# All large tiles 48 bytes past the weights modulo 256

## The chip, the cores and the metric

The kernel runs on one core of one Trainium2 chip. The metric is the device time of one execution in microseconds; three runs of the kernel before gave 1348.78 (median), 1347.21 and 1349.9 us. The runs themselves thus lie within 0.2% of each other.

## What is computed

One inference step of a streaming encoder layer for 256 prompt tokens and 32 sample tokens, which the kernel keeps side by side as 288 columns. The reference, cut to the parts that set the work:

```python
h = rmsnorm(x, norm_in)
(a_q, a_k, a_v, i_q, i_k, i_w, a_z, b_z, b_xbc, b_dt, m_q, m_z, gates) = split_cols(h @ w_in)
...
ya = dsa_attention(...) * jax.nn.silu(a_z)
yb, conv_state, h_last = mamba_branch(b_z, b_xbc, b_dt, ...)
ym = mem_attend(m_q, mem_k, mem_v) * jax.nn.silu(m_z)
g_a, g_b, g_m = jnp.split(jax.nn.sigmoid(gates), N_BRANCH, axis=-1)
merged = g_a * (ya @ w_pa) + g_b * (yb @ w_pb) + g_m * (ym @ w_pm)
return x + merged @ w_o, (k_new, v_new, i_k, conv_state, h_last)
```

Before it, 256 memory tokens are normalised and multiplied by `w_mem_kv`. Everything is float32. All weights together are some 207 MB (395 loads of 512 KB), each read once.

## The kernel before

**Products of three terms.** Each float32 operand of a large product is split into a high part, rounded to the matmul's input format (`F32R`), and a low part, the rest. A product is then high by high, low by high and high by low, accumulated in PSUM: three matmuls for each 128x128 block of weights. The weights are the stationary operand, the 288 token columns the moving one.

**Strips.** `strip` makes 128 output channels. Its weights come in halves of 8 blocks (512 KB): SyncE loads them into `wr` (line 217), ScalarE rounds them into `wh` (line 231), VectorE writes the rest into `wl` (line 232), with three buffers of each (`wpool`). `convert` issues these for the next half while TensorE works on the present one. The 24 matmuls of a half stand in this order: for the rows 0, 2, 4, 6, 1, 3, 5, 7 of the moving tile first `wh` by the high row and `wh` by the low row, then, with the rows in the opposite order, `wl` by the high row. A weight load precedes each matmul, so while a matmul streams its moving row, the weights of the next one are loaded.

**Which tiles are high and low rows.** `xh` and `xl` hold the normed input for `w_in`; slots E and F hold the gated outputs of the memory branch and of attention (`ym`, `ya`), A and B that of the Mamba branch (`yb`), `xh` and `mgl` (in the place of `xl`) the merged result for `w_o`. In the stage of the memory tokens, B and C hold the memory rows (256 columns); there `mv_block` has the memory as the stationary operand and 512 columns of weights as the moving one.

**Side work.** Attention, the scan and the norms are generators that run a step after each half; their matmuls write the PSUM tiles `sd`, those of the strips `ps`. All matmuls are issued by `mm` (line 78).

**Addresses.** A row of a moving tile is 1152 bytes long, four and a half times 256; the two halves of a weights tile (even and odd blocks) lie 2176 bytes apart, eight and a half times 256, and a block is 512 bytes. A row and the weights of the same parity thus have the same distance modulo 256 throughout a tile. `slot` shifts a tile by SHIFT bytes behind its start in the pool. Where the tiles start, modulo 256, as the built programs place them (per partition):

| tile | before | after |
|---|---|---|
| `wh`, `wl` (start of the first block) | 224 | 80 |
| high rows: `xh`, A, E | 128 | 128 |
| low rows: `xl`/`mgl`, B, F | 160 | 128 |
| memory rows in B and C | 160 | 16 |
| high rows minus weights | 160 | 48 |
| low rows minus weights | 192 | 48 |
| memory rows minus weights | 192 | 192 |

Of the kernel before, what the change touches and what calls it, by code (L numbers as in the profile page):

```python
# [7 lines left out]
F32 = mybir.dt.float32  # L8
F32R = mybir.dt.float32r
# [4 lines left out]
P = 128  # L14
# [19 lines left out]
def step_kernel(ctx, tc, ins, outs):  # L34
# [4 lines left out]
    const = ctx.enter_context(tc.tile_pool(name="const", bufs=1))  # L39
    wpool = ctx.enter_context(tc.tile_pool(name="wpool", bufs=3))  # L40
# [20 lines left out]
    def st(n=8):  # L61
        return stp.tile([P, n], F32, tag="st", name="st")

    SHIFT = {"A": 160, "B": 32, "E": 224, "F": 32}

    def slot(tag, shape, dt=F32):

        o = SHIFT.get(tag, 0) // 4
        n = {"E": 2304, "F": 2304, "G": 2304, "H": 2304}.get(tag, 4608)
        t = big.tile([P, n + o], dt, tag=tag, name=tag)  # L70
        m = 1
        for d in shape[1:]:
            m *= d
        t = t[:, o:o + m]
        return t if len(shape) == 2 else t.rearrange("p (a b) -> p a b", a=shape[1])
# [4 lines left out]

    N = Names()
    N.memraw = slot("A", [P, 16, 256])
    N.memh = slot("B", [P, 16, 256], F32R)
    N.meml = slot("C", [P, 16, 256], F32R)
    N.x = slot("D", [P, 16, T])
    def high():
        return const.tile([P, 4616], F32R, name="xh", tag="xh")[:, 0:4608].rearrange("p (k t) -> p k t", k=16)

    xh = high()
    xl = const.tile([P, 16, T], F32R, name="xl", tag="xl")  # L90
    X = (xh, xl)
# [2 lines left out]
    g_mem = const.tile([P, 16], F32, name="g_mem")  # L94
    S.dma_start(g_mem, ins["cols"][:, 0:16])
    nc.sync.dma_start(N.memraw[:, 0:1], ins["memT"][:, 0:1])
    cols = const.tile([P, 288], F32, name="cols")
    g_in, g_ssm, g_fin, d_col = (cols[:, 16 * i:16 * i + 16] for i in range(1, 5))
    cw = cols[:, 80:176].rearrange("p (c i) -> p c i", c=24)
    cbias = cols[:, 176:200]  # L100
# [103 lines left out]
    def convert():  # L204
        i = state["c"]
        if i >= len(jobs):
            return
        state["c"] += 1
        ap, shape, go = jobs[i]
        if ap is None:  # L210
            if shape == "now":
                go()
            else:
                conv.append((None, None, go))
            return convert()
        raw = wpool.tile(shape, F32, tag="wr", name="wr")
        nc.sync.dma_start(raw, ap)
        wh = wpool.tile([P, 1088], F32R, tag="wh", name="wh")
        wl = wpool.tile([P, 1088], F32R, tag="wl", name="wl")
        if shape == [P, 8, P]:  # L220


            wh, wl = (bass.AP(tensor=w.tensor, offset=w.offset, ap=[w.ap[0], [544, 2], [P, 4], [1, P]])
                      for w in (wh, wl))
            raw = raw.rearrange("p (k e) c -> p e k c", e=2)
        elif len(shape) == 3:
            wh, wl = (w[:, 0:shape[1] * shape[2]].rearrange("p (a b) -> p a b", b=shape[2]) for w in (wh, wl))
        else:
            wh, wl = (w[:, 0:shape[1] * shape[2] * shape[3]].rearrange("p (a b c) -> p a b c", a=shape[1], b=shape[2])
                      for w in (wh, wl))  # L230
        S.activation(wh, raw, AF.Copy)  # L231
        V.tensor_tensor(wl, raw, wh.bitcast(F32), OP.subtract)  # L232
        conv.append((wh, wl, go))
# [56 lines left out]
    def run():  # L290
        while conv:
            wh, wl, go = conv.pop(0)
            if wh is None:
                go()
                continue
            convert()
            go(wh, wl)
            step()
# [114 lines left out]

    mem_split(0, 1)
    convert()
    mem_load(1, 1)
    mem_split(1, 1)
    convert()
    mem_load(2, 2)
    mem_split(2, 2)  # L420
# [694 lines left out]
    def begin_pb():  # L1115
        N.mg = (high(),
                const.tile([P, 16, T], F32R, name="mgl", tag="xl"))
# [149 lines left out]
```

## Time and profile before

| | |
|---|---|
| median of three runs | 1348.78 us |
| the profiled execution | 1347.85 us, its span 1346.1 us |
| TensorE matmul busy | 1328.0 us, 99% of the span |
| TensorE weight loads busy | 1296.4 us, 96% |
| VectorE, ScalarE, GpSimd busy | 57%, 46%, 16% |
| granted TensorE clock | 0.997 of full on the mean |
| HBM traffic | 171 GB/s over the span |

[...]

### The profile page before, as it was taken

The page shows a single profiled execution, that of the slowest core. Times are in us where ns is not written, and L with a number is a line of the kernel's source. Part 1 is how long each engine was busy: PE and PEld are TensorE (multiplying, and loading weights), DVE is VectorE, ACT ScalarE, POOL GpSimd, SP SyncE. Part 2 cuts the span into 40 slices and gives each one's busy share as a digit, 9 for nine tenths or more (in the row PEclk, how much of TensorE's full clock was granted, in tenths as well). Part 3 has the DMA queues.
Part 4 walks back from the last instruction along what each step waited for, and adds up shares of the span by engine and source line. Part 5 has one row for each costly group of instructions (what it writes and reads, how often), then busy time and mean ns, then how long its engine had stood idle before and what let it go on. Part 6 is the DMA issues. An engine that isn't in the chain of part 4 may idle for free.

```text
span 1346.1 us, 24533 instructions
## 1 busy us (share of the span) xinstructions
PE 1328.0 (99%) x10102; PEld 1296.4 (96%) x10102; DVE 763.2 (57%) x1175; ACT 624.3 (46%) x871; POOL 209.0 (16%) x291
## 2 busy tenths in 40 slices
PE   9999999999999999999999999999999999999996
PEld 9889999899999999999999999999999999999995
DVE  6874434584577767646566546763344444555444
ACT  6654443444555544735435346664333434334331
POOL 0001000000012212122231234510012000000552
PEclk9999999999999999999999999999999999999998
DMA  8767343344444444655546444444446544445442
GB/s 296 259 210 259 131 141 126 130 157 171 158 142 145 154 157 165 227 168 175 186 141 193 167 163 166 160 169 172 162 169 233 172 167 172 167 164 173 169 162 100
DMA packets 64815, 232.05 MB, mean 172 GB/s; under 512 B 7552, under 2 KB 8224, under 8 KB 63424
## 3 DMA queue, kind: packets, MB, share of 16 engines
q1 hardware_dynamic: 60800, 212.25, 45.7%
q0 software_dynamic: 3328, 16.91, 3.7%
q8 instruction: 79, 1.29, 0.4%
q10 hardware_dynamic: 576, 1.34, 0.3%
q14 instruction: 32, 0.26, 0.1%
HBM read 223.06 MB, written 7.33 MB: 171 GB/s over the span
## 4 chain that ended last, share of the span: by engine, by line
PE 93%; DVE 2%; DMA 2%; issue 1%; ACT 1%; DVEq 0%; SPq 0%; ACTq 0%
PE ps L78 85%; PE sd L78 7%; DMA wr<-in_w_mk 2%; DVE wl L232 1%; ACT wh L231 1%; PE sd L932 0%; DVE A L1161 0%; DVE ev L385 0%; PE sd L798 0%; PE sd L506 0%; PE sd L916 0%; ACT t L661 0%; DVE E L346 0%; DVE t L610 0%; DVE xl L141 0%
## 5 line engine op out<-in xcount | busy, mean ns | idle before, releaser
L232 DVE TENSOR_TENSOR wl<-wr,wh 128x1024 fp32r<-128x1024 f32 (+1 forms) x395 | 487.3, 1235 | 539.9 <-ACT wh L231 530.3
L231 ACT ACTIVATE wh<-wr 128x1024 fp32r<-128x1024 f32 (+1 forms) x395 | 416.2, 1056 | 598.3 <-PE ps L78 467.1
L78 PE MATMUL ps<-xh,wh 128*128 128x288 f32 x2384 | 644.4, 298 | 0.0
L78 PE MATMUL ps<-xl,wh 128*128 128x288 f32 x2128 | 567.0, 293 | 0.2 <-DVE xl L141 0.2
L78 PEld LDWEIGHTS ps<-xh,wh 128*128 128x128 f32 x2384 | 448.7, 188 | 7.5 <-issue 5.5
L78 PEld LDWEIGHTS ps<-xl,wh 128*128 128x128 f32 x2128 | 401.4, 189 | 1.7 <-issue 0.7
L78 PE MATMUL ps<-xh,wl 128*128 128x288 f32 x2384 | 361.0, 293 | 0.0
L78 PEld LDWEIGHTS ps<-xh,wl 128*128 128x128 f32 x2384 | 327.8, 188 | 0.0
L78 PE MATMUL ps<-B,wh 128*128 128x288 f32 (+1 forms) x320 | 77.0, 291 | 0.0
L78 PE MATMUL ps<-E,wh 128*128 128x288 f32 x256 | 69.2, 298 | 0.0
L78 PE MATMUL ps<-A,wh 128*128 128x288 f32 x256 | 68.3, 294 | 0.0
L78 PE MATMUL ps<-mgl,wh 128*128 128x288 f32 x256 | 68.2, 293 | 0.0
L78 PE MATMUL ps<-F,wh 128*128 128x288 f32 x256 | 68.2, 293 | 0.0
L861 POOL COPY cso<-t 128x3 f32<-128x3 f32 x24 | 23.1, 961 | 237.8 <-ACT t L859 237.8
L78 PEld LDWEIGHTS ps<-B,wh 128*128 128x128 f32 x320 | 56.3, 189 | 0.0
L78 PEld LDWEIGHTS ps<-E,wh 128*128 128x128 f32 x256 | 48.2, 188 | 1.1 <-issue 0.8
L78 PEld LDWEIGHTS ps<-F,wh 128*128 128x128 f32 x256 | 48.3, 189 | 0.2 <-issue 0.2
L78 PEld LDWEIGHTS ps<-mgl,wh 128*128 128x128 f32 x256 | 48.3, 189 | 0.0
L78 PEld LDWEIGHTS ps<-A,wh 128*128 128x128 f32 x256 | 48.2, 188 | 0.0
L78 PE MATMUL ps<-E,wl 128*128 128x288 f32 x256 | 38.7, 293 | 0.0
L78 PE MATMUL ps<-A,wl 128*128 128x288 f32 x256 | 38.7, 293 | 0.0
L78 PEld LDWEIGHTS ps<-E,wl 128*128 128x128 f32 x256 | 35.2, 188 | 0.0
(302 smaller groups left out, 1149.1 us busy)
## 6 DMA issues: line engine op xcount, KB each, us to landing
wr<-in_w_in SPq DMA_DIRECT2D x266, 512.0 KB, 3.3
wr<-in_w_pb SPq DMA_DIRECT2D x32, 512.0 KB, 3.3
wr<-in_w_o SPq DMA_DIRECT2D x32, 512.0 KB, 3.2
wr<-in_w_mv SPq DMA_DIRECT2D x16, 512.0 KB, 4.3
wr<-in_w_pm SPq DMA_DIRECT2D x16, 512.0 KB, 3.2
wr<-in_w_pa SPq DMA_DIRECT2D x16, 512.0 KB, 3.2
wr<-in_w_mk SPq DMA_DIRECT2D x15, 512.0 KB, 5.1
B<-scr POOLq DMA_DIRECT2D x4, 1152.0 KB, 9.6
```

What stands on the lines that cost most here:

```text
L78: PE.matmul(out, lhsT, rhs, start=start, stop=stop)
L231: S.activation(wh, raw, AF.Copy)
L232: V.tensor_tensor(wl, raw, wh.bitcast(F32), OP.subtract)
L861: G.tensor_copy(cso[:, c, 0:3], u[:, 256:259])
```

## The change

The weights tiles are read and written from their fifth element on (16 bytes in), the pads of the slots go except one of 64 bytes before A, that of `xh` goes, and `cols` grows by 128 bytes, all of which moves what is allocated behind them. The memory rows in B and C are taken from the slots' 37th element on. No instruction is added, removed or moved on any engine; only addresses differ.

```diff
-    SHIFT = {"A": 160, "B": 32, "E": 224, "F": 32}
+    SHIFT = {"A": 64}
...
-    N.memh = slot("B", [P, 16, 256], F32R)
-    N.meml = slot("C", [P, 16, 256], F32R)
+
+    N.memh, N.meml = (slot(t, [P, 4608], F32R)[:, 36:4132].rearrange("p (k t) -> p k t", k=16) for t in "BC")
...
-        return const.tile([P, 4616], F32R, name="xh", tag="xh")[:, 0:4608].rearrange("p (k t) -> p k t", k=16)
+        return const.tile([P, 4608], F32R, name="xh", tag="xh")[:, 0:4608].rearrange("p (k t) -> p k t", k=16)
...
-    cols = const.tile([P, 288], F32, name="cols")
+    cols = const.tile([P, 320], F32, name="cols")
...
-        wh = wpool.tile([P, 1088], F32R, tag="wh", name="wh")
-        wl = wpool.tile([P, 1088], F32R, tag="wl", name="wl")
+        wh = wpool.tile([P, 1088], F32R, tag="wh", name="wh")[:, 4:1060]
+        wl = wpool.tile([P, 1088], F32R, tag="wl", name="wl")[:, 4:1060]
```

## Rows read from the trace of the kernel before

**Rows 1.** The page: engine, busy us, share, instructions; then the granted clock.
```profile
PE 1328.0 (99%) x10102; PEld 1296.4 (96%) x10102; DVE 763.2 (57%) x1175; ACT 624.3 (46%) x871; POOL 209.0 (16%) x291
...
PEclk9999999999999999999999999999999999999998
```

**Rows 2.** The chain that ended last: shares by line, then its pieces (start, us).
```profile
PE ps L78 85%; PE sd L78 7%; DMA wr<-in_w_mk 2%; DVE wl L232 1%; ACT wh L231 1%; PE sd L932 0%; DVE A L1161 0%; DVE ev L385 0%; PE sd L798 0%; PE sd L506 0%; PE sd L916 0%; ACT t L661 0%; DVE E L346 0%; DVE t L610 0%; DVE xl L141 0%
...
279.38 69.23 PE ps L78 x528
...
884.97 446.88 PE ps L78 x3408
```

**Rows 3.** The page's costliest groups: matmuls of 288 columns, with their counts.
```profile
L78 PE MATMUL ps<-xh,wh 128*128 128x288 f32 x2384 | 644.4, 298 | 0.0
L78 PE MATMUL ps<-xl,wh 128*128 128x288 f32 x2128 | 567.0, 293 | 0.2 <-DVE xl L141 0.2
...
L78 PE MATMUL ps<-xh,wl 128*128 128x288 f32 x2384 | 361.0, 293 | 0.0
...
L78 PE MATMUL ps<-E,wh 128*128 128x288 f32 x256 | 69.2, 298 | 0.0
```

**Rows 4.** Groups by form in 885 to 1331 us: busy us, mean ns.
```profile
L78 PE MATMUL ps<-xh,wh 128*128 128x288 f32 x752 | 200.8, 295 | 0.0
L78 PE MATMUL ps<-xl,wh 128*128 128x288 f32 x496 | 132.1, 293 | 0.0
L78 PE MATMUL ps<-xh,wl 128*128 128x288 f32 x747 | 113.1, 293 | 0.0
L78 PE MATMUL ps<-B,wh 128*128 128x288 f32 x256 | 68.2, 293 | 0.0
```

**Rows 5.** Single low-row matmuls: groups by form at 563.76, 564.46, 564.72, 565.64 us.
```profile
L78 PE MATMUL ps<-xl,wh 128*128 128x288 f32 x1 | 0.3, 298 | 0.0
...
L78 PE MATMUL ps<-xl,wh 128*128 128x288 f32 x1 | 0.3, 290 | 0.0
...
L78 PE MATMUL ps<-xl,wh 128*128 128x288 f32 x1 | 0.3, 294 | 0.0
...
L78 PE MATMUL ps<-xl,wh 128*128 128x288 f32 x1 | 0.3, 291 | 0.0
```

**Rows 6.** The same at 1008.53 and 1008.79 us, then at 1326.34 and 1326.60 us.
```profile
L78 PE MATMUL ps<-F,wh 128*128 128x288 f32 x1 | 0.3, 290 | 0.0
...
L78 PE MATMUL ps<-F,wh 128*128 128x288 f32 x1 | 0.3, 293 | 0.0
...
L78 PE MATMUL ps<-mgl,wh 128*128 128x288 f32 x1 | 0.3, 290 | 0.0
...
L78 PE MATMUL ps<-mgl,wh 128*128 128x288 f32 x1 | 0.3, 293 | 0.0
```

**Rows 7.** Two consecutive `wl` matmuls each, at 566.03 and 566.16 us.
```profile
L78 PE MATMUL ps<-xh,wl 128*128 128x288 f32 x2 | 0.4, 294 | 0.0
...
L78 PE MATMUL ps<-xh,wl 128*128 128x288 f32 x2 | 0.4, 293 | 0.0
```

**Rows 8.** Groups by form at 30 to 39.5 us, 42 to 52 us, 60 to 95 us.
```profile
L78 PE MATMUL ps<-B,wh 128*128 128x256 f32 x26 | 3.6, 276 | 0.0
...
L78 PE MATMUL ps<-B,wh 128*128 128x256 f32 x27 | 3.8, 281 | 0.0
...
L78 PE MATMUL ps<-wh,B 128*128 128x512 f32 x24 | 9.4, 392 | 0.0
L78 PE MATMUL ps<-wl,B 128*128 128x512 f32 x26 | 7.1, 391 | 0.0
```

**Rows 9.** Groups of VectorE, then ScalarE, at 900 to 1300 us, and a DMA issue.
```profile
L232 DVE TENSOR_TENSOR wl<-wr,wh 128x1024 fp32r<-128x1024 f32 x127 | 155.6, 1225 | 210.9 <-ACT wh L231 206.2 <-ACT D L1111 2.3 <-ACT H L1093 2.3
...
L231 ACT ACTIVATE wh<-wr 128x1024 fp32r<-128x1024 f32 x128 | 135.4, 1058 | 212.1 <-PE ps L78 180.6 <-issue 27.3 <-DMA wr<-in_w_in 4.0
...
wr<-in_w_in SPq DMA_DIRECT2D x266, 512.0 KB, 3.3
```

**Rows 10.** SyncE's DMA queue: what it waited for (us in total, times, longest).
```profile
SPq L217 <- DVE wl L232: 973.8, 340, 6.4
```

## The prediction

> **What bounds the kernel.** [...] Next the chain that ended last: 85% of it is one line, the strips' matmuls into `ps`, and hardly a wait for another engine stands in it [rows 2]. So what a strip matmul costs is what the kernel costs, and the question is what sets that cost. The length of a record does not tell it, since records overlap; the pieces of the chain do. One holds 3408 matmuls in 446.88 us, another 528 in 69.23 us: 131.1 ns from start to start in both [rows 2]. [...] In the first of these stretches the records are 293 to 295 ns long on the mean [rows 4]; a record is thus its interval plus 162.5 ns, and I turn the lengths of single records into intervals with that.
>
> Nothing else is near the bound. A half strip (24 matmuls) takes 24 x 131.1 = 3147 ns. For it ScalarE needs 1058 ns and VectorE 1225 ns [rows 9], and both wait for TensorE; SyncE's loads wait for the buffers to come free, 340 times [rows 10], not for data: a load lands 3.3 us after its issue [rows 9], with three buffers to hide it. Even intervals of 127 ns, 3048 ns a half, leave these covers in place.
>
> **The change part by part.** No instruction is added, removed or moved, so no queue, no wait and no buffer changes. Three things move: the distance of moving rows to weights, the start of `wh` and `wl` for the engines that write them, and the start of most small tiles.
>
> The small tiles (`t2`, `ev`, the attention and scan tiles) and the DMA targets shift by multiples of 16 bytes. I cost that at nothing. What hides it is TensorE's lead: VectorE is busy 57% and ScalarE 46% [rows 1]. If their work on a half rose by a fifth, some 0.46 us, 2.28 would become 2.74 us, still below 3.05 us. The side matmuls are 7% of the chain [rows 2]; they keep their mutual distances for the greater part, and I leave them.
>
> The distance is the change. The matmuls of 288 columns number 8688: 2384, 2128 and 2384 in the three big groups and seven groups of 256 (one of the seven stands in [rows 3]). While one streams its row, the next one's weights are loaded, so the distance that can matter is the row streaming now minus the weights loading now. In a half of 24 it is, before, 160 for the high rows and 192 for the low ones, with two exceptions where the order passes between even and odd rows: the low row 6 meets weights of the other parity and stands at 64, and in the `wl` part one high row stands at 32. After the change 22 of the 24 stand at 48, the two exceptions at 176. So 8688 x 22/24 = 7964 intervals change their distance to 48, and 724 move to a place between the two that they know, which I cost at nothing.
>
> No row has 48. All distances of the large tiles before are multiples of 32, and 48 is an odd multiple of 16. The nearest on either side are just the two exceptions. At 64 the record is 290 ns [rows 5, 6] (the second row of the one, the first and third of the other), which is an interval of 127.5 ns; it is so in each of the three tile pairs, while the next low row, two starts later, has 293 or 294, 130.5 to 131.5 ns. At 32 there are only means of two, since `wl` records of one group overlap: 294 with the record before it and 293 with the one behind [rows 7], which makes some 131 ns; I take 130.5 for it, since the pair's other half stands at 160 and high. Between 127.5 and 130.5 I take the middle, 129.0, because 48 is as far from the one as from the other. **The sum:** (131.1 - 129.0) x 7964 = 16.7 us less. The end at 64's value is 3.6 x 7964 = 28.7 us less, the end at 32's value 0.6 x 7964 = 4.8 us less. Against the profiled execution, 1347.85 us (its span is 1346.1; the rest lies around it and stays), that is 1331.1, with 1319.2 and 1343.1 as ends. The median of the runs is 0.9 us above the profiled one, so the forecast is **1332 us**, in its own case 1314 to 1344.
>
> [...]
>
> **The rivals.** *The distance is not what sets the interval.* The low rows at one and the same distance, 192, show 298, 294 and 291 ns [rows 5], so place in the sequence counts as much as distance; and in the memory stage, at 192 throughout and with the same code, the record goes from 276 to 281 ns after a short pause at 40 us and stays there [rows 8]. [...] That speaks for a rhythm between loads and streams into which the engine falls whatever the addresses. The time would be 1348 us, within 0.2% (the measure of what can be told from no change here). [...] *The change does not do what it says* is no case apart: the built addresses do stand at 48.
>
> [...]
>
> **How the numbers follow.** Faster by way of a shorter interval: 0.50, since the two nearest distances in the same sequence both lie at or below the mean. The same: 0.22, for the rhythm that ignores the addresses. Slower: 0.28, for the only steady run at a near distance, which has the largest excess of all. Likeliest is the first, 1332 us. The range runs from 1314 to 1366: it leaves out some 0.03 below and the upper half or a little more of the slower case, 0.16. Faster by over 0.2% (below 1346.1) 0.50, within 0.2% 0.22, slower 0.28.
>
> **What would show it.** In the profile after, the chain's long piece of 3408 matmuls should last 3408 x 129.2 = 440 us in place of 446.88, and the records of all 288-column groups should be some 291 ns; low row 6 should lose its short record. [...] VectorE's and ScalarE's lengths for `wl` and `wh` should stay at 1225 and 1058 ns; if they moved much, the start at 80 would count for itself. In the memory stage nothing should change, its distance being the same; if the records of 276 ns there become 281 or the reverse, the rhythm is set by something other than the distance. The prediction is wrong if the records of the `wl` part, where all have one distance before and after, do not move with those of the `wh` part.

## The result, and the profile after

The changed kernel takes 1360.3 us (median of four runs, 1359.98 to 1361.2) where the kernel before takes 1348.0 (1347.11 to 1349.9): a ratio of 1.0084, interval 1.0072 to 1.0096. It is 12 us slower; the forecast was some 16 us faster. The range, 1314 to 1366 us, does hold the time, but on the side of the rival that I gave 0.28.

The page of the profiled execution after: its span, engines (busy us, share, instructions), granted clock, and the groups that answer to [rows 1, 3] (busy us, mean ns of one record, idle before).

```profile
span 1358.3 us, 24529 instructions
...
PE 1338.0 (99%) x10102; PEld 1306.7 (96%) x10102; DVE 763.0 (56%) x1175; ACT 625.7 (46%) x871; POOL 209.1 (15%) x291
...
PEclk9999999999999999999999999999999999999998
...
L78 PE MATMUL ps<-xh,wh 128*128 128x288 f32 x2384 | 648.9, 298 | 0.0
L78 PE MATMUL ps<-xl,wh 128*128 128x288 f32 x2128 | 571.8, 295 | 0.2 <-DVE xl L141 0.2
...
L78 PE MATMUL ps<-xh,wl 128*128 128x288 f32 x2384 | 365.0, 295 | 0.0
```

TensorE is busy 10.0 us longer with the same 10102 matmuls, and the span is 12.2 us longer. The granted clock has not moved: it is 0.997 of full on the mean in both. VectorE and ScalarE are busy as long as before, to within 1.4 us, and their groups at 900 to 1300 us, answering to [rows 9], have the lengths of before to the nanosecond:

```profile
L232 DVE TENSOR_TENSOR wl<-wr,wh 128x1024 fp32r<-128x1024 f32 x127 | 155.6, 1225 | 211.2 <-ACT wh L231 211.1
...
L231 ACT ACTIVATE wh<-wr 128x1024 fp32r<-128x1024 f32 x127 | 134.4, 1058 | 208.5 <-PE ps L78 174.7 <-issue 28.3 <-DMA wr<-in_w_in 5.2
```

So no engine got more work, and the time is in the matmuls themselves. The pieces of the chain that ended last show how much each takes (start us, us, what).

```profile
280.92 69.96 PE ps L78 x528
...
892.42 451.58 PE ps L78 x3408
```

Before, the long piece took 446.88 us [rows 2]; now 451.58. That is 132.5 ns from start to start in place of 131.1, and the piece of 528 says the same (69.96/528 = 132.5). The difference, (451.58 - 446.88)/3408 x 8688 = 12.0 us, is nearly the whole loss. Two smaller differences beside it almost cancel: TensorE idles some 2.1 us longer in the first 60 us (the span grew by 12.2 us, its busy time by 10.0), and the matmuls of the memory stage and of the side work take 1.7 us less, by their starts in the two traces. That idle time lies between 2.1 and 4.3 us in the nine traces of whole kernels, of fast and slow layouts alike; why it varies was not tested.

The groups by form at 892 to 1332 us, answering to [rows 4], then two low rows, answering to the second and third of [rows 5] (565.60 and 565.87 us).

```profile
L78 PE MATMUL ps<-xh,wh 128*128 128x288 f32 x725 | 194.9, 295 | 0.0
L78 PE MATMUL ps<-xl,wh 128*128 128x288 f32 x496 | 133.2, 295 | 0.0
L78 PE MATMUL ps<-xh,wl 128*128 128x288 f32 x720 | 110.2, 295 | 0.0
L78 PE MATMUL ps<-B,wh 128*128 128x288 f32 x256 | 68.8, 295 | 0.0
...
L78 PE MATMUL ps<-xl,wh 128*128 128x288 f32 x1 | 0.3, 294 | 0.0
...
L78 PE MATMUL ps<-xl,wh 128*128 128x288 f32 x1 | 0.3, 298 | 0.0
```

The records of the low rows (`wh` part) and those of the `wl` part have both grown by 2 ns; those of the high rows in the `wh` part have stayed at 295. Low row 6 has lost its short record (290 before, 294 now). So the addresses do act. But the stage of the memory tokens has changed too, where weights and rows kept their distance of 192 (groups by form at 30 to 39.5, 42 to 52 and 60 to 95 us):

```profile
L78 PE MATMUL ps<-B,wl 128*128 128x256 f32 x27 | 3.7, 275 | 0.0
...
L78 PE MATMUL ps<-B,wh 128*128 128x256 f32 x32 | 4.4, 279 | 0.0
L78 PE MATMUL ps<-C,wh 128*128 128x256 f32 x31 | 4.2, 275 | 0.0
L78 PE MATMUL ps<-B,wl 128*128 128x256 f32 x24 | 3.2, 275 | 0.0
...
L78 PE MATMUL ps<-wh,B 128*128 128x512 f32 x25 | 9.7, 388 | 0.0
L78 PE MATMUL ps<-wl,B 128*128 128x512 f32 x28 | 7.5, 388 | 0.0
```

After the short pause only five records are still some 281 ns (with a first one of 363 they raise the mean of one group to 279); the others are 275 or 276. Those of 512 columns have fallen from 391 or 392 to 388 ns [rows 8]. That was the sign, named ahead, that something other than the distance sets the interval. The experiments ask what.

### The profile page after: what moved, and what is told of

It is laid out like the page before. It is cut to its first block, busy times and chain, and to the rows that moved or that the text cites. A ratio compares the mean times of both kernels' runs of the same rounds, so it can differ in the third digit from the quotient of the medians.

```text
span 1358.3 us, 24529 instructions
## 1 busy us (share of the span) xinstructions
PE 1338.0 (99%) x10102; PEld 1306.7 (96%) x10102; DVE 763.0 (56%) x1175; ACT 625.7 (46%) x871; POOL 209.1 (15%) x291
## 4 chain that ended last, share of the span: by engine, by line
PE 93%; DVE 2%; DMA 2%; issue 1%; ACT 1%; DVEq 0%; SPq 0%; ACTq 0%
PE ps L78 85%; PE sd L78 7%; DMA wr<-in_w_mk 2%; DVE wl L232 1%; ACT wh L231 1%; PE sd L932 0%; DVE A L1161 0%; DVE ev L385 0%; PE sd L798 0%; PE sd L506 0%; PE sd L916 0%; ACT t L661 0%; DVE E L346 0%; DVE t L610 0%; DVE xl L141 0%
## 5 line engine op out<-in xcount | busy, mean ns | idle before, releaser
L78 PE MATMUL ps<-xh,wl 128*128 128x288 f32 x2384 | 365.0, 295 | 0.0
L78 PEld LDWEIGHTS ps<-xh,wl 128*128 128x128 f32 x2384 | 332.9, 189 | 0.0
L78 PEld LDWEIGHTS ps<-A,wl 128*128 128x128 f32 x256 | 35.8, 189 | 0.0
```

Source lines behind the costliest of these rows:

```text
L78: PE.matmul(out, lhsT, rhs, start=start, stop=stop)
```

## The experiments

Each kernel below differs from the kernel before in addresses alone, unless it is said. A layout is written as three starts modulo 256, **weights / high rows / low rows**; the kernel before is 224/128/160 and the change 80/128/128. The memory rows keep their distance of 192 to the weights throughout. The diffs of u64 and u160 are against the changed kernel, those of the others against the kernel before, cut to the lines that set the starts (`wl` goes with `wh`). Times are medians, ratios are against the kernel before on the same chip, and the interval is from the chain's piece of 3408 strip matmuls.

| kernel | layout | distances | us | ratio (95%) | ns from start to start |
|---|---|---|---|---|---|
| before | 224/128/160 | 160, 192 | 1348.0 | 1 | 131.1 |
| after | 80/128/128 | 48, 48 | 1360.3 | 1.0084 (1.0072 to 1.0096) | 132.5 |
| u64 | 64/128/128 | 64, 64 | 1352.9 | 1.0030 (1.0020 to 1.0041) | 131.4 |
| u160 | 224/128/128 | 160, 160 | 1366.1 | 1.0132 (1.0117 to 1.0147) | 133.1 |
| w80 | 80/128/160 | 48, 80 | 1353.0 | 1.0032 (1.0021 to 1.0044) | 131.7 |
| h48l192 | 80/128/16 | 48, 192 | 1355.9 | 1.0056 (1.0041 to 1.0071) | 132.6 |
| s16 | 240/144/176 | 160, 192 | 1362.4 | 1.0103 (1.0088 to 1.0118) | 132.8 |
| d144 | 0/144/144 | 144, 144 | 1347.5 | 0.9990 (0.9981 to 0.9999) | 130.8 |
| d96 | 48/144/144 | 96, 96 | 1343.7 | 0.9963 (0.9949 to 0.9976) | 130.6 |

### u64 and u160: one distance for all rows

u64 is the changed kernel with the weights 16 bytes earlier (and the memory rows with them), so that all rows stand at 64:

```diff
-    N.memh, N.meml = (slot(t, [P, 4608], F32R)[:, 36:4132].rearrange("p (k t) -> p k t", k=16) for t in "BC")
+    N.memh, N.meml = (slot(t, [P, 4608], F32R)[:, 32:4128].rearrange("p (k t) -> p k t", k=16) for t in "BC")
...
-        wh = wpool.tile([P, 1088], F32R, tag="wh", name="wh")[:, 4:1060]
+        wh = wpool.tile([P, 1088], F32R, tag="wh", name="wh")[:, 0:1056]
```

> The kernel after with one edit: the weights start at 64 modulo 256 in place of 80, so that all rows of 288 columns lie 64 past them in place of 48; the memory rows move along and keep 192. Three theories of why the kernel after is slower (132.5 ns a strip matmul in place of 131.1, 12 us). Odd lines: a distance that is an odd multiple of 16 bytes costs 1.4 ns an interval, even ones do not; then 131.1 ns and about 1348 us. One distance for both: what costs is that high and low rows have the same distance; then 132.5 ns and about 1360 us. Each distance has its own price: then neither need hold, and the time is anywhere, by the exception at 64 in the kernel before 127.5 ns and about 1317 us, by the run of 512 columns at 64 about 135 ns and 1385 us.

u160 puts the weights where they were before and all rows at 128. It is thus also one part of the change alone: of the large tiles only the low rows move, from 160 to 128.

```diff
-    SHIFT = {"A": 64}
+    SHIFT = {"A": 192}
...
-        wh = wpool.tile([P, 1088], F32R, tag="wh", name="wh")[:, 4:1060]
+        wh = wpool.tile([P, 1088], F32R, tag="wh", name="wh")[:, 8:1064]
```

> The layout of the kernel after, but the weights start at 224 as before, so that all rows lie 160 past them, as the high rows did before; the memory rows keep 192. Odd lines: 131.1 ns a strip matmul, about 1348 us. One distance for both: 132.5 ns, about 1360 us. Each distance has its own price: the second part of a half in the kernel before, eight high rows at 160 one behind the other, takes some 131 ns each, so about 131 ns and 1348 us by this theory too.

The long pieces of the chain, first of u64:

```profile
888.67 447.79 PE ps L78 x3408
```

then of u160:

```profile
896.88 453.46 PE ps L78 x3408
```

The exception at 64 that looked like 127.5 ns in the kernel before [rows 5, 6] costs 131.4 ns once every row stands there (447.79/3408). And 160, at which the high rows of the kernel before have always stood, costs 133.1 ns when the low rows stand there too. One distance in a mixed sequence does not have the price that it has in a uniform one. The two simpler theories fall with these runs: by odd lines both kernels would take about 1348 us, by one distance for both about 1360 us, and they take 1352.9 and 1366.1. The 135 ns that the third theory takes from the run of 512 columns no run shows.

u160 shows a second thing, in the stage of the memory tokens, whose addresses modulo 256 are those of the kernel before. Its groups by form at 30 to 39.5 and at 42 to 52 us:

```profile
L78 PE MATMUL ps<-B,wl 128*128 128x256 f32 x24 | 3.3, 281 | 0.0
...
L78 PE MATMUL ps<-B,wl 128*128 128x256 f32 x24 | 3.2, 276 | 0.0
```

Before it was 276 first and 281 after the pause [rows 8]; here it is 281 first and 276 after. The same matmuls with the same alignment run in either of two rhythms, and which one is not fixed by the alignment.

### s16: the distances of before, every start 16 bytes later

```diff
-    SHIFT = {"A": 160, "B": 32, "E": 224, "F": 32}
+    SHIFT = {"A": 208, "B": 16, "E": 208, "F": 16}
...
-    xl = const.tile([P, 16, T], F32R, name="xl", tag="xl")
+    def low(name):
+        return const.tile([P, 4616], F32R, name=name, tag="xl")[:, 4:4612].rearrange("p (k t) -> p k t", k=16)
+    xl = low("xl")
...
-        wh = wpool.tile([P, 1088], F32R, tag="wh", name="wh")
+        wh = wpool.tile([P, 1088], F32R, tag="wh", name="wh")[:, 12:1068]
...
```

> The kernel before with all its distances (160, 192 and 192 for the memory) but every start moved by 16 bytes: weights at 240, high rows at 144, low rows and memory at 176. If only distances count, nothing changes: 131.1 ns, 1348 us within 0.2%. If it is the start at an odd multiple of 16 bytes, as that of the weights after, that costs: 132.5 ns and 1360 us, with the distances of before.

The page's line on the engines and the long piece of the chain of s16:

```profile
PE 1340.5 (99%) x10102; PEld 1309.5 (96%) x10102; DVE 761.9 (56%) x1175; ACT 626.9 (46%) x871; POOL 210.7 (16%) x291
...
891.94 452.51 PE ps L78 x3408
```

With 160 and 192 kept, the interval is 132.8 ns and the kernel 14 us slower. So the distance alone, on which the prediction was built, does not set the interval. VectorE and ScalarE are as busy as before (761.9 and 626.9 us, against 763.2 and 624.3), so their writes to the shifted tiles take no longer; whether these writes slow TensorE is left to b1.

### w80 and h48l192: the change in parts

w80 moves the weights to 80 and leaves the low rows at 160; h48l192 moves the low rows as well, to 16, so that they keep their distance of 192.

```diff
-    SHIFT = {"A": 160, "B": 32, "E": 224, "F": 32}
+    SHIFT = {"A": 64, "B": 32, "E": 224, "F": 32}
...
-        wh = wpool.tile([P, 1088], F32R, tag="wh", name="wh")
+        wh = wpool.tile([P, 1088], F32R, tag="wh", name="wh")[:, 4:1060]
```

> The weights' part of the change alone: weights at 80 as after, high rows at 128 and low rows at 160 as before, so distances of 48 and 80; the memory rows keep 192. Reads alone (the interval is a function of both distances and of the start of the weights): the time follows the interval that the same layout has with nothing but the strips' matmuls, which the run beside this one measures; by the mean of all layouts so far, 132.4 ns, about 1360 us. Change undone in half (each half of the change carries half of its cost): 1354 us. The low rows at 48 carry the whole cost: 1348 us.

The added lines of h48l192 (its `low` starts a low tile 144 bytes into what is allocated):

```diff
+    SHIFT = {"A": 64, "B": 144, "E": 96, "F": 144}
...
+        return const.tile([P, 4656], F32R, name=name, tag="xl")[:, 36:4644].rearrange("p (k t) -> p k t", k=16)
...
+        wh = wpool.tile([P, 1088], F32R, tag="wh", name="wh")[:, 4:1060]
...
```

> Half of the change: the high rows lie 48 past the weights as after, the low rows 192 as before. Odd lines: two thirds of the intervals (the high rows) keep the cost of 1.4 ns, so 132.0 ns a strip matmul and about 1356 us. One distance for both: the distances differ again, so 131.1 ns and 1348 us. Each distance has its own price: between the two, by 48 alone 132.0 ns.

The long piece, first of w80, then of h48l192:

```profile
889.51 448.75 PE ps L78 x3408
```

```profile
887.51 452.05 PE ps L78 x3408
```

Moving the weights alone costs 4.6 us (1353.0 against 1348.4 in the same runs), moving the low rows alone (u160) 17.6 us, and both together, which is the change, 12.3 us. The parts do not add up: the price of a place for the low rows depends on where weights and high rows stand. w80 lies where "change undone in half" put it (1354), but the 17.6 us of the other half refute that rule. h48l192 has no one interval at all. Within the long piece its half strips take 3176 and 3191 ns in turn, by the starts of their matmuls, while 74 half strips elsewhere in the kernel take 3146 or 3147 ns, as in the kernel before: again several rhythms under one alignment. So the 132.6 ns of the table hold for its long piece only, and that its time, 1355.9 us, meets the 1356 of odd lines is luck.

### b1 to b3: the strips' matmuls alone

To see whether any other engine has a hand in it, and to try many layouts at once, these kernels keep nothing but the 48 matmuls of a strip, in their order, on tiles filled once. No load, no rounding and no side work runs beside them.

```diff
+    for w, h, l in LAYOUTS:
+        vh, vl = weights(wh, w // 4), weights(wl, w // 4)
+        hi, lo = rows(xh, h // 4), rows(xl, l // 4)
...
+                for i in ORDER:
+                    PE.matmul(p, vh[:, i % 2, i // 2], hi[:, 8 * j + i], start=j == 0 and i == 0, stop=False)
+                    PE.matmul(p, vh[:, i % 2, i // 2], lo[:, 8 * j + i], start=False, stop=False)
+                for i in ORDER[::-1]:
+                    PE.matmul(p, vl[:, i % 2, i // 2], hi[:, 8 * j + i], start=False, stop=j == 1 and i == 0)
```

> The strips' matmuls by themselves: TensorE alone, with nothing that writes SBUF while it works (no ScalarE, VectorE or DMA work on weights, no side work; the outputs are not computed). For each of 60 layouts (start of weights, high rows and low rows modulo 256) three strips of 48 matmuls in the kernel's order, a short float32 matmul ahead of each strip. Two theories. Reads alone: what sets the interval is how the streaming rows and the weight loads meet, so each known layout gives what it gives in the kernel: 131.1 ns for that of before, 132.6 for that of after, 131.4 with weights at 64, 133.0 for one distance of 160, 132.8 for the starts of before moved by 16. Writers: what costs are the writes of ScalarE, VectorE and the DMAs into the same memory; then without them all layouts take the same time, less than 131.1 ns.

In the chain of b1 the eight `wl` matmuls of a half make one piece (line 86). From the first half's piece to the second half's there are 24 intervals. The pieces of one strip each, in the layouts of before, after, u64, u160 and s16 in turn:

```profile
32.01 1.05 PE ps L86 x8
35.16 1.05 PE ps L86 x8
...
58.30 1.07 PE ps L86 x8
61.50 1.07 PE ps L86 x8
...
77.96 1.05 PE ps L86 x8
81.11 1.05 PE ps L86 x8
...
97.77 1.07 PE ps L86 x8
100.97 1.07 PE ps L86 x8
...
137.29 1.07 PE ps L86 x8
140.48 1.07 PE ps L86 x8
```

35.16 - 32.01 is 3.15 us, 131.1 ns an interval by the unrounded times. The others are 3.20 (133.0), 3.15 (131.4), 3.21 (133.6) and 3.19 us (132.8). That is the order of the whole kernels, and the sizes agree within 0.6 ns. TensorE alone reproduces the effect, with no other engine at work.

From here on a figure for a layout is the mean of the 46 intervals of a strip from its second matmul on, by the unrounded starts. The first strip of each kernel is left out: its first matmuls start 240 ns apart.

b1 also moved the layout of before through all sixteen starts. At the eight even multiples of 16 bytes a strip's interval was 130.9 to 132.1 ns, mostly 131.1 or less; at the eight odd ones 132.8 to 133.0, without exception. The distances were the same all along.

One layout does not always give one figure. Of the 112 layouts that have more than one strip in b1 to b3, half have strips within 0.2 ns of each other, but those of 26 lie 0.5 ns or more apart, those of 5 lie 1.0 ns or more apart, and the widest 1.7. The layout of h48l192, for one, has strips of 131.3 and of 132.7 ns, as the whole kernel has both. A figure from a single strip can thus be off by half a nanosecond or more.

b2 and b3 have the same code with other lists: b2 all 256 pairs of distances at weights of 64 and the sixteen uniform ones at 80, b3 rows at every pair of multiples of 32 with the weights at 80.

> The strips' matmuls alone again (nothing else is computed): one strip of 48 matmuls for each of 272 layouts. With the weights at 64, every pair of distances of high and low rows in steps of 16 bytes; then, with the weights at 80, an odd multiple of 16, one distance for both in 16 steps. Theory of distance and start: the interval is a function of both distances and of whether the weights start at an even or odd multiple of 16, so 48 gives 132.1 ns with weights at 64 and 133.0 with weights at 80, as the run before has them, and the other distances differ between the two starts as well. Theory of distance alone: the two series of one distance agree to 0.2 ns. [...]

> The strips' matmuls alone (nothing else is computed), two strips for each layout: weights at 80, high and low rows at every pair of multiples of 32, then the layouts of after, of weights at 64 and of before. Reads alone: the pair 128, 160 gives what the full kernel with that layout gives, to 0.3 ns; after 133.0, before 131.1 as in the first of these runs. If the kernel before stands near the best of all layouts, few or none of these 64 lie below 131.1 ns and their mean is near 132.4.

The pieces of b2 for the uniform distances 32 and 144 (weights at 64), then 96 (weights at 80):

```profile
247.66 1.06 PE ps L86 x8
250.87 1.06 PE ps L86 x8
...
1030.91 1.05 PE ps L86 x8
1034.05 1.05 PE ps L86 x8
...
1747.99 1.05 PE ps L86 x8
1751.12 1.05 PE ps L86 x8
```

3.21, 3.14 and 3.13 us; over the whole strip 133.6, 130.8 and 130.6 ns. Over the 255 pairs that are left the interval runs from 130.8 to 134.3 ns, its mean is 132.4, and the distances of the kernel before (131.1) come eighth, each by one strip. No pair comes near the 126.8 ns that the lower end of the prediction's range asks for ((1348 - 1314)/7964 is 4.3 ns less than 131.1). A uniform 48 has 132.7 with weights at 64 and 132.6 at 80. The expected split, 132.1 and 133.0, did not come; b1 had 132.0 to 132.4 and 133.0 for the same two layouts, so the spread between strips hides it. With the weights at 64, uniform 64 costs 131.5 and uniform 32 costs 133.6; with the weights at 80 they cost 132.4 and 133.0. In b3 no layout is below 131.1, and the mean is 132.4. Its two strips of the layout of w80 have 132.1 and 132.2 where the whole kernel has 131.7, which is more than the 0.3 ns that were allowed.

So the cause is not a start of one operand alone. In b1, rows and weights that move together by 32 bytes at a time mostly keep the 131.1 ns; in b2, rows that move against the weights by as much do not (uniform 32, 64 and 96 cost 133.6, 131.5 and 131.8). It lies in where the two operands start against each other, and the even or odd start counts beside it (130.9 to 132.1 and 132.8 to 133.0 ns in b1, at the same distances).

### d96 and d144: two distances taken from the list

d96 takes the uniform 96 with all starts at odd multiples of 16, d144 the uniform 144 with even ones. The starts themselves are others than in b2 (48/144/144 for 80/176/176, and 0/144/144 for 64/208/208), so that these kernels also try whether distance and parity are enough. To find room, `xh` and `xl` share one tile, in which the merged result takes their place, and a pool of small tiles has 10 buffers in place of 12.

```diff
-    stp = ctx.enter_context(tc.tile_pool(name="stp", bufs=12))
+    stp = ctx.enter_context(tc.tile_pool(name="stp", bufs=10))
...
-    SHIFT = {"A": 160, "B": 32, "E": 224, "F": 32}
+    SHIFT = {"A": 112, "B": 240, "E": 240, "F": 240}
...
+    both = const.tile([P, 9224], F32R, name="xh", tag="xh")
+    xh, xl = (both[:, o:o + 4608].rearrange("p (k t) -> p k t", k=16) for o in (4, 4612))
...
+        wh = wpool.tile([P, 1088], F32R, tag="wh", name="wh")[:, 4:1060]
+        wl = wpool.tile([P, 1088], F32R, tag="wl", name="wl")[:, 4:1060]
...
```

> The best single layout that the strips alone have shown: weights at 48, all rows of 288 columns at 144, so one distance of 96 with every start at an odd multiple of 16 (130.6 ns there, in one strip; before 131.1). High and low rows share one tile for that, and one small pool has 10 buffers in place of 12; the memory rows keep 192. Reads alone: 0.5 ns less on 8688 matmuls, 4.5 us, and up to 1 us in the memory stage, whose starts are odd as after: 1343 us, ratio 0.996. Before as the least that addresses can give: 1348 us or more. An odd start of the weights is what made the kernel after slow: 1360 us.

> As the run beside it, but the weights at 0, an even start, and so one distance of 144: 130.9 ns in the strips alone (five strips of the earlier runs, 130.8 to 131.0). Reads alone: 0.2 ns less than before on 8688 matmuls, 2 us: 1346 us, ratio 0.9985. One distance for both as the cause: 1360 us.

The span, the engines' line and the long piece of the chain of d96:

```profile
span 1342.0 us, 24533 instructions
...
PE 1321.7 (98%) x10102; PEld 1290.1 (96%) x10102; DVE 763.8 (57%) x1175; ACT 624.8 (47%) x871; POOL 208.8 (16%) x291
...
882.71 444.96 PE ps L78 x3408
```

The long piece of d144:

```profile
885.35 445.90 PE ps L78 x3408
```

130.6 ns an interval in d96, as b2 had it at other starts; (446.88 - 444.96)/3408 x 8688 = 4.9 us less, and the span is 4.1 us shorter. d96 beats both kernels, at 1343.7 us (against 1349.3 in the same runs). So an odd start of the weights is not slow by itself, nor is one distance for all rows. For d144, 130.8 ns would give 2.5 us; measured are 1.8 (1347.5 against 1349.3), with a ratio whose interval ends just below 1. Neither shared tile nor smaller pool shows in the page of d96: the other engines are as busy as before.

## Why the prediction was wrong

**The bound** was read rightly. The kernel costs what its strip matmuls cost: 8688 times the change in the interval is 12.0 us where the span grew by 12.2, and across the nine layouts the order of the intervals is nearly the order of the times (h48l192, whose long piece is slower than its other stretches, breaks it).

**What the change moves** was right in kind. The loss is in the spacing of the strip matmuls, but for the smaller differences that nearly cancel. ScalarE's and VectorE's lengths stayed (1058 and 1225 ns), and the small tiles' moves cost nothing that can be seen. The records of the `wl` part moved with those of the low rows, so the sign that would have refuted the distance theory did not come.

**The step that failed is the price of 48.** I took 127.5 ns for a distance of 64 and 130.5 for 32, both from single exceptions in a sequence that otherwise stood at 160 and 192, and put 48 in their middle at 129.0. u64 and b2 show what these distances cost when they are steady: 131.4 or 131.5 ns at 64, 133.6 at 32. The middle of these would be 132.5, just what 48 gave; but that may be chance, since the series over the distances is not smooth and is another one with weights at 80. A short interval in a periodic sequence is a part of that period: low row 6's 290 ns stood among low rows of 298, 294 and 291 ns at one and the same distance [rows 5], so that the interval varied by more within one distance than between the two that I compared. The 291 is low row 7, which stands at 192: by the starts in the long piece of the kernel before, the interval behind it is 127.2 ns on the mean, and that behind low row 6, at 64, 127.1. The short interval was thus no mark of 64, and the trace before could show it. In u64, where nearly every row stands at 64, most of each half runs in a cycle of four intervals of 135.0, 133.3, 131.7 and 126.7 ns: even a steady distance has no price for one matmul, only a rhythm with a mean. I cited the rows for a rival and did not let them bear on the term. The lower end of the range, 1314 us, takes 4.3 ns off the interval, a term that no run shows: the least that any layout had on the mean, 130.6 ns in b2 and in d96, is 0.5 ns below 131.1.

**The second fault is the variable itself.** The distance is not what sets the interval: s16 keeps both distances and loses 14 us. Three starts count together: the distances and, as far as shifts were tried, whether the starts are even or odd multiples of 16 bytes.

**The slower rival**, a steady distance that costs more than the mixture, was right for this change (132.5 ns against 131.1), though not as a rule: d96 is steady and the fastest (130.6), s16 is mixed and slow (132.8). Its chance rests on the largest excess of an interval over the time of its columns. That time no run shows at the strips' pace, and so neither the excess nor the upper end of the range, 1366 us, that came of it; what the runs showed in its place is 1.4 ns more an interval, 12 us. And the steady run that the chance names, the matmuls of 512 columns in the memory stage, is itself a matter of the start: its records fell from 391 or 392 to 388 ns with the distance unchanged.

**The rival that the addresses do not matter** falls. In b1, matmuls that are the same but for their addresses take 130.9 to 133.9 ns an interval, with no other engine at work. But its observation that the engine falls into a rhythm is borne out: u160 runs the memory stage in the two rhythms of the kernel before, in the opposite order (records of 281 ns, then 276).

**What a random layout costs** was never asked, and it would have spoken against the forecast. Against b2's mean of 132.4 ns the kernel before stood 1.3 ns low, which is 1.3 x 8688 = 11 us. From a layout near the best, most changes of the layout lead upwards; 247 of the other 254 pairs were worse. Before the change this could not be read from the one trace.

**Open** is how the rhythm comes about: why 96 with starts at odd multiples of 16 gives 130.6 ns and 160 there 132.6, and why some layouts hold several rhythms. The runs show that the cause lies in where TensorE's two operands start; they do not show how. Of the 4096 layouts at steps of 16 bytes 359 were tried alone, and whether one is below 130.6 was not.

## What to carry to other kernels

A duration that stands once in a periodic, back-to-back sequence is not the price of its operands; price an edit only by a steady run of the very thing, and where the trace has none, keep both signs open. When the bound is one engine's own spacing and the edit only moves addresses, a kernel of that engine's instructions alone can price hundreds of layouts in one run, and here its figures held in the whole kernel within 0.6 ns, apart from one layout that has two figures. It needs several strips of each layout. Starts of both operands are worth such a search (130.6 to 134.3 ns, 2.8%), but the gain over a layout already chosen is small: 0.4%.

## What the runs showed of the hardware that was not expected

Where the operands start in SBUF changes the spacing of back-to-back matmuls with a weight load each: 130.6 to 134.3 ns for 288 columns.

At the head of b1, b2 and b3, in three layouts, this difference is missing: the first matmuls start 240 ns apart, to the nanosecond, before the interval falls to some 131 to 134 ns. From b1, in us:

```profile
21.23 0.44 PE L83 MATMUL ps<-xh,wh 128*128 128x288 f32 x1
21.47 0.44 PE L84 MATMUL ps<-xl,wh 128*128 128x288 f32 x1
21.71 0.44 PE L83 MATMUL ps<-xh,wh 128*128 128x288 f32 x1
```

The kernel before has such a head too, by the starts in its trace: its matmuls of 256 columns start 213.4 ns apart from 5.70 to 6.77 us, and 113.3 ns apart from 7.03 us on. The trace's record of the granted clock begins between the two, at 6.80 us, with full. 213.4 x 288/256 is 240.1 ns, so that the heads of b1 to b3 run at the pace of that stretch is an estimate from these intervals. Their pages do not show the clock that was granted there.

Whether the starts are even or odd multiples of 16 bytes matters by itself. For 512 columns all the kernels with the weights at 0, 64 or 224 have records of 390 to 392 ns on the mean, and all those with weights at 48, 80 or 240 have 388, at one and the same distance. There the odd start is the faster one; for the strips at the distances of before it is the slower one (132.9 against some 131.1 ns).

At 256 columns and even starts two rhythms exist under one alignment, with records of 276 and 281 ns, and the slower one lasts: for 94 matmuls or more in a row in three of the four kernels with even starts. In the five with odd starts it is left after five at most, by the starts in their traces. What decides between the two did not show.
